# Weighted sum of eight index heads: fp32 matmuls against diagonal weights in place of scalar-tensor operations

## The chip, the cores and the metric

The kernel runs on one core of one Trainium2 chip. The metric is the device time of one execution in microseconds; the median of the runs is quoted. A core has a matrix engine (TensorE, PE in the profile), a vector engine (VectorE, DVE), a scalar engine (ScalarE, ACT), a general engine (GpSimd, POOL) and a queue that issues DMAs (SyncE, SP). Each works through its own list of instructions in order; semaphores make one wait for another. Matmuls write to PSUM, from which DVE and ACT read.

## The reference, cut to what matters

The program is a two-layer decoder trunk on 1024 tokens of 1024 features: an RWKV-7 time mixing and a gated convolution FFN, then sparse attention and a second such FFN. Only the attention is touched. For each of eight blocks of 128 queries it scores all keys with eight small index heads, keeps the 256 best keys of each query, and attends to those:

```python
s_idx = jnp.einsum('bthd,bsd->bths', qi_b, k_idx)
score = jnp.einsum('bths,bth->bts', jax.nn.relu(s_idx), wi_b).astype(jnp.float32)
causal = key_pos[None, :] <= t_pos[:, None]
score = jnp.where(causal[None], score, -jnp.inf)
_, sel = lax.top_k(score, topk)
...
logits = jnp.einsum('bthc,btkc->bhtk', q_abs, kv_sel).astype(jnp.float32) * qk_scale
```

`wi_b` holds one weight for each query and index head. The second line, the sum over the heads h of weight times relu, is what the change computes in another way. `topk` is 256, so the blocks 0 and 1 (tokens 0 to 255) keep every key and need no scores.

## The kernel before, in words

The attention (`dsa`) holds queries on the 128 partitions and keys along the free dimension. Block b sees W = 128 (b + 1) keys. `indexer(b)` scores blocks 2 to 7: for each slice of up to 512 keys and each head, PE makes two fp32r products into one PSUM bank (tile `si`, lines 1471 and 1472), ACT writes its Relu to SBUF (`relu`, line 1474), and DVE multiplies it with the head's weight column of `widx` and adds it to the scores `sc` (line 1476 for the first head, line 1478 for the seven others). POOL then masks future keys (`affine_select`, line 1482).

`topk` finds the 256th best score of each query by a binary search in two halves of 16 steps each, first on the upper 16 bits of the scores (tile `top`), then on the lower (tile `low`). It handles two blocks side by side: of one, DVE counts the keys above the limit (line 1515); of the other, ACT does (line 1513). After each count DVE moves the limit (lines 1517 and 1518). Between the two halves stand some twenty small operations (lines 1520 to 1544).

`logits` makes four heads' logits on PE (`lg`), and DVE adds the mask (`cm`, from POOL at line 1622) and takes the row minimum (`p`, `mn`, line 1638); ACT takes the exponential (line 1643). `values` transposes the probabilities on PE (`tp`, line 1669), ACT copies them out (`ph`, line 1677), PE multiplies by the values in plain fp32 (`ol`, line 1682) and by the output weights (`ops`, line 1687). `qabs` prepares the queries of 256 tokens (`qa`). Scores, logits and `qa` take turns in four PSUM banks of tag `l`.

The main line is attention in 32 units of four heads. Beside it a generator mixes in the rest: blocks 2, 3 and 4 are scored first, then units 0 to 6 run with the selection of blocks 2 and 3, block 5 is scored, units 7 to 14 run with the 32 head steps of blocks 6 and 7 and the selection of blocks 4 and 5, and units 15 to 22 run with the selection of blocks 6 and 7. The order in which instructions stand on each engine is made by a scheduler with a cost model of its own, from the order in which the program emits them and the buffers that are free.

The code below is that of the kernel before.

Of the kernel before, what the change touches and what calls it, by code (L numbers as in the profile page):

```python
# [30 lines left out]
class Ctx:  # L31
    """Handles shared by the phases."""


class Rows:
    """A [1024, 1024] DRAM array held as tiles of 128 rows."""

# [12 lines left out]
def split(k, raw, hi, lo, hi_eng="a", lo_eng="p"):  # L50
    """raw = hi + lo, each within float32r's digits."""
    nc = k.nc
    if hi_eng == "a":
        nc.scalar.copy(hi, raw)  # L54
    elif hi_eng == "v":
        nc.vector.tensor_copy(hi, raw)
    else:
        nc.gpsimd.tensor_scalar(hi, raw, 1.0, 0.0, ALU.mult, ALU.add)
    eng = nc.vector if lo_eng == "v" else nc.gpsimd
    eng.tensor_tensor(lo, raw, f32(hi), ALU.subtract)  # L60
# [9 lines left out]
def rstd_of(k, pool, var, n, eps, scale=1.0, tag="rs"):  # L70
    """(var * scale + eps) ** -0.5 on [128, n]"""
    nc = k.nc
    ve = pool.tile([128, n], F32, name="ve", tag=tag + "v", bufs=2)
    nc.vector.tensor_scalar(ve, var, scale, eps, ALU.mult, ALU.add)
    rs = pool.tile([128, n], F32, name="rs", tag=tag + "r", bufs=2)
    nc.gpsimd.tensor_tensor(rs, ve, k.mhalf[:, :n], ALU.pow)
    return rs


def layer_norm_rows(k, pool, res, g, b, out, eng="pp", sums=None, junk=None):  # L80
    """out[128, 1024] = LN(res) * g + b; res and out are lists of two [128, 512] tiles, sums [128, 2] the sums of res if
    they are known."""
    nc = k.nc
# [36 lines left out]
def wsplit(k, u, ap, n=512, lo_eng="v", raw=None):  # L120
    """DRAM block [128, n] -> hi, lo tiles"""
    raw = (raw or u)("wr")[:, :n]
    lo, hi = u("wl", F32R)[:, :n], u("wh", F32R)[:, :n]
    k.nc.sync.dma_start(raw, ap)
    split(k, raw, hi, lo, "a", lo_eng)
    return hi, lo


def out_z(k, acc, Z, z, g):
    """Feature-major hi, lo [128, 4, 512] of a 512-token half's g-th 512 features; z(tt, g) are token-major tiles."""  # L130
    zt = [z(tt, g) for tt in range(4)]
# [8 lines left out]
def residual(k, r, src, row, ch, ps):  # L140
    """r = ALPHA * src rows + ps"""
    k.nc.sync.dma_start(r, src[row : row + 128, ch * 512 : (ch + 1) * 512])
# [9 lines left out]
def out_proj(k, pool, u, raw, acc, res_tile, Z, w_ap, src, dst, hf, lnw):  # L152
    """dst rows of a 512-token half = LN(ALPHA * src + z @ w), Z = the two out_z of it; a generator of 16 products and
    4 normalisations."""
    res = {}
# [19 lines left out]
def out_proj_last(k, pool, u, raw, acc, acc1, wlate, nlate, res_tile, Z, w_ap, src, dst, hf, lnw):  # L175
    """out_proj whose rows are finished one tile of tokens after the other; Z[1] is only used after the third step.
    wlate has room for the split weights of the last nlate products."""
    a = {}
# [44 lines left out]
def interleave(main, n, *sides):  # L223
    """n steps of main with m steps of each (side, m) spread between them."""
    done = [0] * len(sides)
# [19 lines left out]
class Pools:  # L245
    """Pools that a phase opens and closes at its own points."""

# [23 lines left out]
def rwkv(k, src, dst):  # L271
# [74 lines left out]
    def mixed(hf, kt, n, xx=None, eng="p"):  # L346
        """hi, lo of x + (shift(x) - x) * mix[n] for one 128-feature tile."""
        xT = st[hf]["xT"]
# [56 lines left out]
    def prefetch(hf, n, g, m):  # L405
        """the first m operands of a projection to come"""
        for kt in range(m):
# [24 lines left out]
    def slot(ap, x):  # L432
        """first (k of BK, a of AR) or second (b of BK, r of AR) half of every 64-token chunk's 128 columns"""
        return ap.rearrange("p (c x i) -> p c x i", x=2, i=64)[:, :, x, :]
# [4 lines left out]
    def lora2(hf, g):  # L439
        """Decay and in-context rate gates; the rate waits in AR's a slots."""  # L440
        h_ = st[hf]
# [42 lines left out]
    def head_sums(ps, src_, i):  # L484
        """Token-major sums of src_ over the two heads of feature tile i."""
        for tt in range(4):
# [67 lines left out]
    def prep(hf, g, half):  # L554
        """Chunk matrices of 512 tokens x 8 heads, and the inverses (I - L)^-1 of their 64 x 64 triangles."""
        s = un[hf, g]
# [278 lines left out]
def ffn(k, layer, src, dst):  # L835
    """Both products go by Strassen-Winograd on 2 x 2 blocks: with
    S1 = A21 + A22, S2 = S1 - A11, S3 = A11 - A21, S4 = A12 - S2, T1 = B12 - B11, T2 = B22 - T1, T3 = B22 - B12,
    T4 = B21 - T2 and U = A11 B11 + S2 T2, V = U + S3 T3, the product's blocks are
    C11 = A11 B11 + A12 B21, C12 = U + S1 T1 + S4 B22, C21 = V + A22 T4, C22 = V + S1 T1."""
    nc, tc = k.nc, k.tc  # L840
# [19 lines left out]

    # x, feature-major: K halves by token halves
    X, raws = {}, {}
# [4 lines left out]
    def x_T(tt, ps):  # L867
        """ps() gives half a token tile's room"""
        pool = P_ if tt < 4 else L_
# [57 lines left out]
    def w_op(f, n, pool=None):  # L927
        """split operand n of the gate and value columns' tiles f"""
        w = W[f]
# [143 lines left out]

    # the second product: pairs of h's tiles, token halves by feature halves
    NPAIR = NF // 2
# [16 lines left out]
    def d_op(p, n, pool, lo_eng):  # L1092
        """operands of product n, both sides: hi and lo [128, 2, 512]"""
        r = R[p]
# [62 lines left out]
    def tail_op(f):  # L1157
        """a tile of h and its rows of the weights"""
        if layer == 1 and f == NF - 1:
# [61 lines left out]
def dsa(k, src, dst):  # L1221
# [41 lines left out]

    # absorbed query weights, scaled: w_uq[:, h] @ w_uk[h]
    wqk = k.dram.tile([8, 2, 128, 512], F32, name="wqk")
# [192 lines left out]
    def indexer(b):  # L1458
        """scores of block b's queries, future keys far below"""
        W = 128 * (b + 1)  # L1460
        s = M_.tile([128, W], F32, name=f"sc{b}")
        sc[b] = s
        lo = 256 if b < 4 else 512
        qs = slice(128 * b - lo, 128 * b - lo + 128)
        for n0 in range(0, W, 512):
            n1 = min(W, n0 + 512)
            n = n1 - n0
            for h in range(8):
                ps = acc("si")
                q_ = QS[lo][:, h, qs]  # L1470
                nc.tensor.matmul(ps[:, :n], q_, XTh[:, 3, n0:n1], start=True, stop=False)
                nc.tensor.matmul(ps[:, :n], q_, XTl[:, 3, n0:n1], start=False, stop=True)
                r = u("relu")
                nc.scalar.activation(r[:, :n], ps[:, :n], AF.Relu)
                if h == 0:
                    nc.vector.tensor_scalar(s[:, n0:n1], r[:, :n], widx[:, b, 0:1], 0.0, ALU.mult, ALU.add)
                else:
                    nc.vector.scalar_tensor_tensor(
                        s[:, n0:n1], r[:, :n], widx[:, b, h : h + 1], s[:, n0:n1], ALU.mult, ALU.add
                    )  # L1480
                yield
        nc.gpsimd.affine_select(
            s[:, W - 128 :], s[:, W - 128 :], pattern=[[-1, 128]], compare_op=ALU.is_ge, fill=-3e38, base=0,
# [5 lines left out]
    def topk(blocks):  # L1489
        """sc[b] <- 0 where the key is among the row's TOPK best, else NEG. The TOPK-th best is found bit by bit: first  # L1490
        the upper, then the lower half of the scores' bits, mapped to integers in the scores' order."""
        tag = f"_{blocks[0]}"
# [11 lines left out]
        def search(s, keys, first, lim):  # L1504
            """16 steps to c = the largest integer with no less than the limit's keys at or above it; the scalar
            engine sums the signs of keys - c + 1/2"""
            W, act, cnt, v = s["W"], s["act"], s["cnt"], s["v"]
# [65 lines left out]
    def qabs(pr, g):  # L1573
        """absorbed queries of 256 tokens, 8 heads: [128 c, hi/lo, head, token]"""
        Q = big("Q", (128, 2, 8, 256))
# [29 lines left out]
    def logits(b, g, g4):  # L1605
        """unnormalised softmax of four heads' logits"""
        W = 128 * (b + 1)
# [42 lines left out]
    def kv_split():  # L1650
        """kv's hi and lo, four key tiles each, in the room of the selection"""
        for i in range(2):
# [71 lines left out]
    def attention(u0, u1, n1):  # L1724
        """values of units u0 .. u1 - 1, logits up to unit n1 - 1"""
        for n in range(u0, u1):
# [48 lines left out]
    def wlate(name, dt=F32):  # L1775
        """a [128, 512] tile of the room that the queries and the probabilities leave"""
        if name == "wr":
# [118 lines left out]
def drive(phases):  # L1896
    """A phase starts (up to its first yield) before the one in front of it ends (from its last yield on)."""
    for i, ph in enumerate(phases):
# [28 lines left out]
```

## Time and profile before

| What | Value |
|---|---|
| device time, median of 3 runs | 3272.94 us (3261.83 to 3287.3) |
| span of the profiled execution, first to last instruction | 3266.9 us (its own total time is not given) |
| PE matmul busy | 2878.4 us, 88% |
| PE weight loads busy | 2257.1 us, 69% |
| DVE busy | 2620.8 us, 80% |
| ACT busy | 1492.1 us, 46% |
| POOL busy | 1718.2 us, 53% |
| first and last score product (line 1472) | 1893.4 and 2121.0 us |

Times within the execution count from its first instruction. Busy time is that of an engine's instructions, overlaps counted once. The table by stretch gives the busy time of PE, of its weight loads, of DVE, ACT and POOL in that order, each with the number of records in brackets, then the granted TensorE clock as a share of full speed. In a timeline a row has the start, the length, the engine, line, operation, tiles (out<-in), shape and the number of records that it merges. A plain fp32 matmul leaves two records.

### The profile page before, as it was taken

The page shows a single profiled execution, that of the slowest core. Times are in us where ns is not written, and L with a number is a line of the kernel's source. Part 1 is how long each engine was busy: PE and PEld are TensorE (multiplying, and loading weights), DVE is VectorE, ACT ScalarE, POOL GpSimd, SP SyncE. Part 2 cuts the span into 40 slices and gives each one's busy share as a digit, 9 for nine tenths or more (in the row PEclk, how much of TensorE's full clock was granted, in tenths as well). Part 3 has the DMA queues.
Part 4 walks back from the last instruction along what each step waited for, and adds up shares of the span by engine and source line. Part 5 has one row for each costly group of instructions (what it writes and reads, how often), then busy time and mean ns, then how long its engine had stood idle before and what let it go on. Part 6 is the DMA issues. An engine that isn't in the chain of part 4 may idle for free. (4 is left out here: it accounts for less than half of the span.)

```text
span 3266.9 us, 41699 instructions
## 1 busy us (share of the span) xinstructions
PE 2878.4 (88%) x15096; PEld 2257.1 (69%) x15096; DVE 2620.8 (80%) x4015; ACT 1492.1 (46%) x2571; POOL 1718.2 (53%) x1105
## 2 busy tenths in 40 slices
PE   6879869988898899999779888888999899999798
PEld 4667647766686677777667766656777677777577
DVE  7897897888847788888876779998475788888965
ACT  4545445454223444444222567876363444444222
POOL 5735445446124676666666622121313676766766
PEclk8889979989889899999889879999999899999889
DMA  2111111112216232236211611112214222235212
GB/s 79 61 40 43 58 36 38 57 33 62 94 56 206 78 84 77 78 83 210 101 65 35 217 40 65 62 33 86 81 51 155 71 78 78 78 91 206 77 52 91
DMA packets 187842, 268.36 MB, mean 82 GB/s; under 512 B 11914, under 2 KB 105482, under 8 KB 187250
## 3 DMA queue, kind: packets, MB, share of 16 engines
q1 hardware_dynamic: 187634, 265.69, 25.2%
q8 instruction: 119, 1.95, 0.2%
q14 instruction: 89, 0.73, 0.1%
HBM read 212.82 MB, written 52.82 MB: 81 GB/s over the span
## 5 line engine op out<-in xcount | busy, mean ns | idle before, releaser
L60 POOL TENSOR_TENSOR wo<-wr,wo 128x512 fp32r<-128x512 f32 x220 | 413.9, 1905 | 284.2 <-ACT wo L54 276.2
L990 DVE SCALAR_TENSOR_TENSOR cv<-u,vec,cv 128x1023 f32<-128x1023 f32 (+1 forms) x176 | 348.0, 1995 | 52.9 <-ACT cv L985 51.1
L60 POOL TENSOR_TENSOR xml<-xm,xmh 128x512 fp32r<-128x512 f32 x132 | 202.0, 1542 | 225.4 <-ACT xmh L54 215.7
L65 PE MATMUL dn<-dh 128*128 128x512 f32 x532 | 221.4, 416 | 66.3 <-DVE acc L1117 66.1
L60 POOL TENSOR_TENSOR dl<-raw,dh 128x1024 fp32r<-128x1024 f32 x82 | 219.2, 2696 | 104.7 <-ACT dh L54 104.4
L66 PE MATMUL dn<-dl,dh 128*128 128x512 f32 x532 | 218.8, 411 | 13.2 <-POOL dl L60 6.7
L65 PE MATMUL p<-xT,wo 128*128 128x512 f32 x528 | 215.1, 407 | 17.1 <-ACT u L974 11.3
L1622 POOL TENSOR_TENSOR cm<-sc,toep 128x256 f32<-128x256 f32 x96 | 75.8, 795 | 293.4 <-DVE mn L1638 225.1
L985 ACT ACTIVATE cv<-u,vec 128x1024 f32<-128x1024 f32 x88 | 109.5, 1244 | 252.7 <-DVE u L979 252.1
L67 PE MATMUL dn<-dh,dl 128*128 128x512 f32 x532 | 218.7, 411 | 0.0
L67 PE MATMUL p<-xT,wo 128*128 128x512 f32 x528 | 210.7, 399 | 4.6 <-POOL wo L60 4.6
L66 PE MATMUL p<-xT,wo 128*128 128x512 f32 x528 | 211.0, 400 | 3.0 <-DVE xT L60 3.0
L1117 DVE SCALAR_TENSOR_TENSOR acc<-acc,dn 128x512 f32<-128x512 f32 x196 | 131.0, 681 | 87.9 <-PE dn L67 87.9
L60 POOL TENSOR_TENSOR wo<-S,wo 128x512 fp32r<-128x512 f32 x88 | 175.4, 2013 | 30.7 <-ACT wo L54 30.7
L54 ACT CAST dh<-raw 128x1024 fp32r<-128x1024 f32 x95 | 94.7, 1046 | 201.7 <-PE dn L67 87.6
L60 POOL TENSOR_TENSOR wl<-wr,wh 128x512 fp32r<-128x512 f32 x84 | 121.6, 1448 | 119.8 <-ACT wh L54 84.8
L65 PEld LDWEIGHTS dn<-dh 128*128 128x128 f32 x532 | 106.0, 199 | 97.2 <-DVE acc L1117 41.5
L54 ACT CAST xmh<-xm 128x512 fp32r<-128x512 f32 x144 | 88.9, 617 | 114.4 <-DVE xm L353 35.5
L65 PE MATMUL p<-x,wo 128*128 128x512 f32 x352 | 139.2, 396 | 1.7 <-DVE x L60 1.3
L65 PEld LDWEIGHTS p<-xT,wo 128*128 128x128 f32 x528 | 100.3, 190 | 57.3 <-ACT u L974 27.2
L54 ACT CAST wo<-wr 128x512 fp32r<-128x512 f32 x220 | 127.2, 618 | 27.2 <-POOL wo L60 18.8
L66 PE MATMUL p<-x,wo 128*128 128x512 f32 x352 | 138.4, 393 | 0.0
(426 smaller groups left out, 9076.6 us busy)
## 6 DMA issues: line engine op xcount, KB each, us to landing
wr<-in_w_up_dram SPq DMA_DIRECT2D x88, 512.0 KB, 5.9
wr<-in_w_rkv_dram SPq DMA_DIRECT2D x96, 256.0 KB, 2.6
hd<-cv SPq DMA_DIRECT2D x44, 512.0 KB, 3.4
raw<-hd SPq DMA_DIRECT2D x19, 1024.0 KB, 4.9
raw<-in_w_down_dram SPq DMA_DIRECT2D x19, 1024.0 KB, 7.9
wr<-in_w_wo_dram SPq DMA_DIRECT2D x68, 256.0 KB, 2.8
acc<-x SPq DMA_DIRECT2D x16, 512.0 KB, 6.1
wh<-wqk SPq DMA_DIRECT2D x32, 256.0 KB, 3.0
```

Source lines behind the costliest of these rows:

```text
L54: nc.scalar.copy(hi, raw)
L60: eng.tensor_tensor(lo, raw, f32(hi), ALU.subtract)
L65: mm(ps, lhs[0], rhs[0], start=start, stop=False, **kw)
L66: mm(ps, lhs[0], rhs[1], start=False, stop=False, **kw)
L67: mm(ps, lhs[1], rhs[0], start=False, stop=stop, **kw)
L985: nc.scalar.activation(o, u, AF.Identity, bias=k.vec[:, cb : cb + 1], scale=k.vec[:, cw[2] : cw[2] + 1])
L990: nc.vector.scalar_tensor_tensor(o[:, d:], u[:, : 1024 - d], k.vec[:, cw[j] : cw[j] + 1], o[:, d:], ALU.mult, ALU.add)
L1117: nc.vector.scalar_tensor_tensor(o, o, ALPHA if first else 1.0, ps, ALU.mult, ALU.add)
L1622: (nc.vector if CFG["cm"][h4] == "v" else nc.gpsimd).tensor_tensor(cm[:, :near], mk, toep[g][:, h % 8, 256 - near :], ALU.add)
```

## The change

The weighted sum goes to PE. For each block POOL builds eight 128x128 diagonal matrices, the identity times one head's weight column, in two tiles `dg` of four (two POOL operations). After the Relu of head h, PE multiplies the diagonal of head h - 2 by that head's Relu, in plain fp32, and accumulates over the eight heads in one PSUM bank (`st`, from the same four banks of tag `l`). After the last head one DVE copy takes the sum to `sc`. The Relu stays on ACT, the mask on POOL. The diff also takes out comments and docstrings all over the file, which moves line numbers below the indexer by 10; it is cut here to the indexer.

```diff
     def indexer(b):
...
+        dg = [qr("dg").rearrange("p (a b) -> p a b", a=4) for _ in range(2)]
+        for i in range(2):
+            nc.gpsimd.tensor_tensor(
+                dg[i], k.ident[:, None, :].to_broadcast([128, 4, 128]),
+                widx[:, b, 4 * i : 4 * i + 4, None].to_broadcast([128, 4, 128]), ALU.mult,
+            )
         for n0 in range(0, W, 512):
             n1 = min(W, n0 + 512)
             n = n1 - n0
+            tot, rs = acc("st"), {}
+
+            def weigh(h):
+                nc.tensor.matmul(tot[:, :n], dg[h // 4][:, h % 4], rs.pop(h)[:, :n], start=h == 0, stop=h == 7)
+
             for h in range(8):
...
-                r = u("relu")
+                r = rs[h] = u("relu")
                 nc.scalar.activation(r[:, :n], ps[:, :n], AF.Relu)
-                if h == 0:
-                    nc.vector.tensor_scalar(s[:, n0:n1], r[:, :n], widx[:, b, 0:1], 0.0, ALU.mult, ALU.add)
-                else:
-                    nc.vector.scalar_tensor_tensor(
-                        s[:, n0:n1], r[:, :n], widx[:, b, h : h + 1], s[:, n0:n1], ALU.mult, ALU.add
-                    )
+                if h >= 2:
+                    weigh(h - 2)
                 yield
+            weigh(6)
+            weigh(7)
+            nc.vector.tensor_copy(s[:, n0:n1], tot[:, :n])
```

The scheduler sets the lists of the engines anew. On DVE, where the first softmax minimum of attention stands (unit 0, `p,mn<-lg,cm`), the list of the kernel before reads as follows; `sc_14783` is block 4's scores, and `cj,cnt` is a count of the search of block 3, on the upper halves (`top`).

```order
L1517 TENSOR_SCALAR v_2_14666<-cnt_2_14665 128x1
L1515 TENSOR_SCALAR cj,cnt_2_14684<-top,c_2_14683 128x512
L1478 SCALAR_TENSOR_TENSOR sc_14783<-relu,widx,sc_14783 128x128
L1518 TENSOR_SCALAR c_2_14664<-v_2_14666,c_2_14664 128x1
L1478 SCALAR_TENSOR_TENSOR sc_14783<-relu,widx,sc_14783 128x128
L1517 TENSOR_SCALAR v_2_14685<-cnt_2_14684 128x1
L1478 SCALAR_TENSOR_TENSOR sc_14783<-relu,widx,sc_14783 128x128
L1638 ISA p,mn<-lg,cm 128x128
```

In the changed list the same place reads as follows, with block 4's scores named `sc_14795` and their sum in PSUM `st`.

```order
L1525 TENSOR_SCALAR cj,cnt_2_14696<-low,c_2_14695 128x512
L1527 TENSOR_SCALAR v_2_14697<-cnt_2_14696,need_2_14702 128x1
L1491 COPY sc_14795<-st 128x128
L1527 TENSOR_SCALAR v_2_14678<-cnt_2_14677,need_2_14683 128x1
L1528 TENSOR_SCALAR c_2_14695<-v_2_14697,c_2_14695 128x1
L1528 TENSOR_SCALAR c_2_14676<-v_2_14678,c_2_14676 128x1
L1648 ISA p,mn<-lg,cm 128x128
```

The accumulation is gone from the list, and the search is further on: it counts on the lower halves (`low`). Before, 11 counts of block 3's search stand ahead of the first minimum; now 21 do.

On PE, at the end of block 7's scores and just ahead of the logits of unit 16, the list of before holds these rows.

```order
L1682 MATMUL ol<-ph,kv 128x512 x2
L1471 MATMUL si<-XTh,QS 128x512
L1472 MATMUL si<-XTl,QS 128x512
L1471 MATMUL si<-XTh,QS 128x512
L1472 MATMUL si<-XTl,QS 128x512
L1687 MATMUL ops<-wuv,ols 128x64 x4
L1471 MATMUL si<-XTh,QS 128x512
L1472 MATMUL si<-XTl,QS 128x512
```

The changed list holds these there.

```order
L1482 MATMUL si<-XTh,QS 128x512
L1483 MATMUL si<-XTl,QS 128x512
L1477 MATMUL st<-relu,dg 128x512
L1482 MATMUL si<-XTh,QS 128x512
L1483 MATMUL si<-XTl,QS 128x512
L1477 MATMUL st<-relu,dg 128x512 x3
L65 MATMUL lg<-XTh,Q 128x512
```

Each head's pair of products is now followed by one weighted product of an earlier head, and the last three stand together ahead of the logits.

## Rows read from the trace of the kernel before

**Rows 1.** busy time by stretch; from:to, length, busy us (records), PE clock, DMA
```profile
1893.00:1947.00 54.00, 40.95 (x188) 31.39 (x187) 45.24 (x136) 35.64 (x87) 6.31 (x8) 0.84 0.18 59
1947.00:1995.00 48.00, 43.88 (x280) 36.46 (x280) 45.50 (x219) 40.25 (x124) 16.82 (x29) 0.93 0.24 83
1995.00:2013.00 18.00, 15.35 (x87) 11.73 (x85) 17.96 (x52) 11.85 (x30) 3.65 (x5) 1.00 0.17 59
2013.00:2132.00 119.00, 98.37 (x480) 68.75 (x480) 116.73 (x424) 92.00 (x209) 27.25 (x35) 0.97 0.14 45
2132.00:2246.00 114.00, 98.16 (x508) 70.58 (x509) 108.19 (x395) 86.96 (x171) 23.18 (x30) 0.96 0.12 38
2380.00:2430.00 50.00, 49.99 (x278) 40.80 (x277) 39.52 (x122) 30.48 (x56) 10.37 (x15) 1.00 0.05 17
```

**Rows 2.** timeline of PE in D; start, length, engine, line, tiles, shape, records
```profile
2106.09 0.39 PE L1471 MATMUL si<-XTh,QS 128*128 128x512 f32 x1
2106.31 0.40 PE L1472 MATMUL si<-XTl,QS 128*128 128x512 f32 x1
...
2111.11 0.60 PE L1669 MATMUL tp<-ident,p 128*128 128x128 f32 x4
2111.54 1.02 PE L1682 MATMUL ol<-ph,kv 128*128 128x512 f32 x2
...
2113.30 1.02 PE L1682 MATMUL ol<-ph,kv 128*128 128x512 f32 x2
2114.16 0.60 PE L1669 MATMUL tp<-ident,p 128*128 128x128 f32 x4
```

**Rows 3.** groups by shape, PE, C and D; xcount, busy us, mean ns, idle
```profile
L1682 PE MATMUL ol<-ph,kv 128*128 128x512 f32 x62 | 33.3, 629 | 5.7 <-ACT ph L1677 5.6
L1669 PE MATMUL tp<-ident,p 128*128 128x128 f32 x120 | 20.1, 283 | 0.3 <-ACT p L1643 0.3
...
L66 PE MATMUL qa<-XTl,wh 128*128 128x256 f32 x34 | 10.0, 295 | 0.0
L1687 PE MATMUL ops<-wuv,ols 128*128 128x64 f32 x72 | 9.7, 278 | 1.8 <-ACT ols L1684 1.6
```

**Rows 4.** busy time by stretch of L1478 alone, then of L1476
```profile
1893.00:1947.00 54.00, 15.84 (x25) 0.84 0.18 59
1995.00:2013.00 18.00, 8.49 (x14) 1.00 0.17 59
2013.00:2132.00 119.00, 21.27 (x28) 0.97 0.14 45
...
1893.00:2246.00 353.00, 4.97 (x10) 0.94 0.15 51
```

**Rows 5.** a copy out of PSUM by shape; instructions of L1420 on POOL
```profile
L341 DVE COPY xT<-pt 128x512 f32<-128x512 f32 x8 | 5.5, 688 | 4.9 <-PE pt L335 4.9
...
L1420 POOL TENSOR_TENSOR toep<-toep,c x8: 1038/1039/1042, 1859.3 to 1935.4; 128x512 f32<-128x512 f32 x8
```

**Rows 6.** instructions of L1472; min/median/max ns, first and last start, shapes
```profile
L1472 PE MATMUL si<-XTl,QS x80: 272/393/628, 1893.4 to 2121.0; 128*128 128x512 f32 x48, 128*128 128x384 f32 x16, 128*128 128x128 f32 x8, 128*128 128x256 f32 x8
```

**Rows 7.** timeline of DVE in A and at the start of B
```profile
1920.02 0.74 DVE L1515 TENSOR_SCALAR_CACHE_REDUCE cj<-top,c 128x512 int16<-128x512 int16 x1
...
1935.37 0.75 DVE L1515 TENSOR_SCALAR_CACHE_REDUCE cj<-top,c 128x512 int16<-128x512 int16 x1
...
1936.59 0.69 DVE L1452 TENSOR_TENSOR QS<-qi,QS 64x512 fp32r<-64x512 f32 x1
...
1947.30 0.29 DVE L1638 CUSTOM_DVE_ANT_0 p<-lg,cm 128x128 f32<-128x128 f32 x1
...
1957.73 0.20 DVE L1518 TENSOR_SCALAR c<-v,c 128x1 f32<-128x1 f32 x1
...
1962.78 0.15 DVE L1544 TENSOR_SCALAR need<-need 128x1 f32<-128x1 f32 x1
```

**Rows 8.** what PE's idle time before L1471 waited for; us, times
```profile
  ACT relu L1474: 8.4, 18
```

More of the change, by code (lines that the diff above doesn't have):

```diff
@@ L31 @@
 class Ctx:
+    pass
 class Rows:
```

## The prediction

> **What bounds the kernel now.** I read the tables by stretch first, then the timelines of VectorE and TensorE, then the groups by shape. Only the attention layer's indexer is edited, and its eighty pairs of score products lie between 1893 and 2121 us [rows 6]. [rows 1] cuts 1893 to 2246 us into five stretches. A (1893 to 1947): query blocks 2, 3 and 4 are scored, and the selection (top-k) of blocks 2 and 3 begins. B (to 1995): attention on blocks 0 and 1. C (to 2013): block 5 is scored. D (to 2132): blocks 6 and 7 are scored head by head between the attention of blocks 2 and 3 and the selection of 4 and 5. E (to 2246): the selection of 6 and 7 beside the attention of 4 and 5. The reader is to see VectorE (DVE) busy 45.50 of 48 us in B, 17.96 of 18 in C, 116.73 of 119 in D and 108.19 of 114 in E: from the first search on it sets the pace. ScalarE (ACT) has 92.00 of 119 in D. PE's busy column reads 98.37 of 119 in D, and this is where the choice of measure matters.
>
> A matmul's row is longer than the place it takes. In [rows 2] two fp32r matmuls of 512 columns read 0.39 us each but start 0.22 apart (0.23 between most); four transposes take 0.43; one fp32 (not fp32r) product of 512 columns is two records and holds PE from 2113.30 to 2114.16, 0.86 us. Counting C and D that way from [rows 3]: 62 records of ol at 0.43 = 26.7; 120 transposes at 0.11 = 13.2; 102 qa (34 on each of three lines; 256 columns, half of 0.23) at 0.12 = 12.2; 72 ops, as short as a transpose, at 0.11 = 7.9; the logits of blocks 2 and 3, sixteen heads each with three products of 384 or 512 columns, 48 x 0.17 + 48 x 0.23 = 19.2, and block 4's first few 2; the score products of blocks 5, 6, 7, (32 x 0.23 + 8 x 0.17 + 8 x 0.12) x 2 = 19.4. Together 101 of 137 us, where the busy column sums to 113.7.
>
> **What it removes, adds and moves.** Removed from DVE: 70 scalar-tensor operations, 15.84 + 8.49 + 21.27 us in A, C and D plus a 1.3 us remainder at the start of B, and 10 tensor-scalar ones, 4.97 us [rows 4]; 51.9 in all. Added to DVE: ten copies of the sums out of PSUM, whose nearest row is a 128x512 copy out of PSUM at 0.69 us [rows 5]: six long ones 4.1, two of 384 columns about 1.1, the 256 and 128 about 0.7; 5.9. Net -46 us of DVE.
> Added to PE: eighty fp32 products with the shapes that [rows 6] lists (48 of 512 columns, 16 of 384, 8 of 256, 8 of 128). At 0.86 for 512 and in proportion: 48 x 0.86 + 16 x 0.65 + 8 x 0.43 + 8 x 0.22 = 41.3 + 10.4 + 3.4 + 1.8 = 57 us. By stretch: A 20.8 (blocks 2, 3, 4), C 10.3, D 25.8. So PE takes on more than DVE gives up.
> Added to POOL: twelve multiplications that build the diagonals; the nearest row, also 128x512 with one operand repeated, is 1.04 us [rows 5], 12.5 us in all. POOL is busy 27.25 of 119 us in D, so I cost them at nothing; if they were late, PE's first product of a block would wait. ACT keeps its eighty Relus.
> New waits: a weighted product waits for the Relu two heads back, and everything behind it on PE waits too; the copy on DVE waits for the block's last product, and the selection steps and softmax minima behind it wait with it. The sum also holds one of the four PSUM banks that scores, logits and qa share.
> Moved: in DVE's list the first softmax minimum (p) of attention now stands behind 21 steps of the search of block 3 where it stood behind 11, and so behind the work between that block's two searches (both lists are shown above). SP keeps its instructions, with a few stores of z a few places away.
>
> Now stretch by stretch.
> A. From the first search step (1920.02) to the first p (1947.30) DVE needed 27.3 us [rows 7]. Off it: block 4's accumulation before p, 11 of A's 25 operations, 15.84 x 11/25 = 7, and its two first heads, 0.5 each [rows 4]. On it: ten more steps at 1.22 (1935.37 to 1936.59), the work between the searches at 4 (1957.73 to 1962.78 less 1 us that belongs to others), two qa splits that used to come earlier 1.4, copies 0.9. 27.3 - 8 + 12.2 + 4 + 1.4 + 0.9 = 37.8: +10.5. The 12.1 us of products for blocks 2 and 3 lie ahead of the search; PE is idle 13 of 54 us in A by its busy column, so I let 2.5 of them through (bounds 0 and 9). A: +13, between +8 and +20.
> B. The ten steps and the work between, 16 us, and the 1.3 are gone from DVE, which leaves 28 of 45.5. PE does what it did: 43.88 by the busy column, about 39 if that shrinks as in C and D (101/113.7). With 40 for the stretch: -7 to -8, I take -7; bounds -9 and -3.
> C and D. DVE: 134.7 - 8.49 - 21.27 - 3 (its share of the 4.97) + 3.6 = 105. PE: 101 + 36 = 137, the whole of the 137 us that the stretches last now. PE becomes the bound. In 2380 to 2430, where nothing else binds, it reads 49.99 of 50 [rows 1]; among the waits for ACT here I expect 95%: 137 / 0.95 = 144, +7. Bounds 0 (no gap at all) and +15 (90%).
> E. No indexer work lies here; a few us of small DVE operations stand earlier in the list now. -3, bounds -6 and 0.
> Sum: 13 - 7 + 7 - 3 = **+10 us**, bounds -7 and +32. After 2246 us PE's order is the one of before. The profiled span is 3266.9, so the sum gives a span of 3277; the shown runs' median, 3272.94, is 6.0 above that span (the profiled execution's own total is not given), so I predict 3283 us.
>
> A rule speaks against counting PE like this. The Trainium skill (Perfetto Trace Analysis, section Identifying the Most-Contended Engine) calls matmul busy share a bad measure of PE's headroom, which the 0.39 against 0.23 bears out, and puts the busy share of weight loads in its place. By the busy column C and D would need 113.7 + 36 = 150 us, +13 instead of +7. By the weight loads, 11.73 + 68.75 of 137 or 59%, PE would have room for all of it and the stretch would follow DVE down to 107 us, -30. I take neither: an fp32 product holds PE 0.86 us for two loads, so loads undercount it.
>
> **Rivals.** (1) *PE packs without gaps.* DVE's relief then shows: A +8, B -9, C and D 0, E -6, so -7: 3266 us. For it: DVE is what PE waited for in the front part, and its load falls by a seventh. Against it: ACT at 92 of 119 stays, and PE waits for ACT more than for DVE there. In the extreme of PE never binding, as weight loads would have it, the sum is 13 - 7 - 30 - 3 = -27: 3246 us.
> (2) *The weighted products stand waiting for ACT* (slower). In D PE's queue is one file of logits, transposes, values and weighted products; a Relu that comes late holds all of it, where before only DVE waited. For it: PE already lost 8.4 us in 18 waits for Relu, 0.47 each [rows 8], and ACT's own queue holds the searches' sign passes. At 0.47 for D's 32 products 15 us are added, 3298; at 1 us each 32, 3315. From about 0.7 us each on it decides the sign beyond what can be told. Against it: between a Relu and its product stand two heads' scores, 0.92 us of PE work, and in A and C a head of 512 columns costs PE 2 x 0.23 + 0.86 = 1.3 us with nothing of attention between, which leaves ACT time for one Relu.
> (3) *Half clock.* A's granted clock is 0.84 [rows 1]; if PE's longer work in A falls in a half-clock span, 14 us of block 4 become up to 28, and A is +20 or more: 3290 us. It is inside the range.
>
> **How the numbers follow.** My forecast, PE bound in C and D and the front part longer, with (3) in it: 0.53, 3276 to 3293. Rival 1: 0.22, of which the extreme has 0.05. Rival 2: 0.22. 0.03 for what I don't see. The range runs from 3255 to 3316: below it lies the extreme of rival 1 and a little more, above it the worst of rival 2. One per cent, 33 us (about what runs of this kernel can tell from no change), puts the borders at 3240 and 3306. Faster by that: 0.04, half of rival 1's extreme and of what I don't see. Slower: 0.16, rival 2 from 0.7 us on and the worst of A. Within: 0.80.
>
> **What would show it.** In the profile after: DVE's operations on the scores gone and ten copies of 0.3 to 0.7 us there; 160 more PE records, 0.43 us apart at 512 columns; first p at about 1960; DVE near 105 of C and D's 144 and PE without idle time; E still DVE's. If D is shorter than 119 us, PE was not the bound and rival 1 holds; if PE shows idle time in front of the weighted products with Relu as the releaser, rival 2. If the first p comes at 1947 or earlier, my reading of DVE's list is wrong.

## The result, and the profile after

The changed kernel took 3318.26 us, median of four runs (3299.45 to 3331.82), against 3267.39 us for the kernel before: a ratio of 1.0127 (the two medians alone give 1.0156), 95% interval 1.0081 to 1.0173, or 26 to 57 us slower. The forecast was 3283 us and 10 us slower: the direction was right, the size a fifth to a quarter of what came; the median lies 2 us above the range's upper end, while the median of the kernel before is here 6 us below the one that the forecast started from.

All of it lies between two points that any profile shows: the start of the second product of the indexer's first pair of score products on TensorE (PE, line 1472 before, 1483 after) and the last softmax minimum on VectorE (DVE, line 1638, then 1648). Call this the stage. The tables below cut it at the first minimum, at block 5's first score product and at the last score product; the four stretches answer to A, B, C with D, and E of the prediction, only that E runs on to the last minimum. Of the profiles below, that of the kernel with blocks 2 to 4 alone is of a slow execution (3315.06 us; its fastest took 3264.9). The columns are those of [rows 1]. First the kernel before, at these cuts:

```profile
1893.40:1947.30 53.90, 40.85 (x188) 31.31 (x186) 45.52 (x136) 35.92 (x89) 6.31 (x8) 0.84 0.18 59
1947.30:1997.60 50.30, 46.14 (x291) 37.87 (x291) 47.83 (x231) 41.88 (x127) 17.55 (x30) 0.93 0.26 87
1997.60:2121.00 123.40, 103.02 (x516) 73.89 (x515) 121.13 (x445) 97.16 (x228) 26.95 (x34) 0.97 0.15 49
2121.00:2445.00 324.00, 292.13 (x1482) 220.37 (x1480) 241.76 (x737) 185.30 (x345) 76.61 (x87) 0.97 0.18 61
```

The changed kernel:

```profile
1891.70:1964.10 72.40, 60.79 (x245) 41.84 (x245) 50.19 (x193) 42.89 (x108) 13.05 (x15) 0.89 0.13 44
1964.10:2016.80 52.70, 48.51 (x307) 40.36 (x307) 35.22 (x167) 37.90 (x114) 17.88 (x31) 0.92 0.24 78
2016.80:2158.70 141.90, 131.55 (x598) 87.65 (x597) 110.73 (x405) 98.08 (x223) 31.98 (x41) 1.00 0.13 44
2158.70:2490.20 331.50, 299.13 (x1488) 225.71 (x1486) 231.11 (x716) 183.74 (x341) 74.33 (x84) 0.95 0.18 59
```

The stage grew from 551.7 to 598.5 us: A +18.5, B +2.4, C and D +18.5, E +7.5. PE's busy column rose by 20 in A and 28.5 in C and D; DVE fell to 110.73 of 141.90 us and no longer fills any stretch.

What one weighted product costs is as forecast. In block 5's scoring, where nothing else is on PE (timeline of PE, columns as [rows 2]):

```profile
2019.92 0.79 PE L1482 MATMUL si<-XTh,QS 128*128 128x512 f32 x1
2020.56 0.39 PE L1483 MATMUL si<-XTl,QS 128*128 128x512 f32 x1
2020.79 1.02 PE L1477 MATMUL st<-relu,dg 128*128 128x512 f32 x2
2021.24 0.80 PE L1482 MATMUL si<-XTh,QS 128*128 128x512 f32 x1
```

A head takes 1.32 us from XTh to XTh; two score products apart by 0.23 leave 0.86 for the weighted one. The 0.64 between XTh and XTl is then part of it: XTl starts late behind it, where two score products follow each other in 0.23 us. The other new operations cost what [rows 5] had, by line (min/median/max ns, first and last start, shapes):

```profile
L1467 POOL TENSOR_TENSOR dg<-ident,widx x12: 1038/1040/1041, 1882.1 to 2113.4; 128x512 f32<-128x512 f32 x12
...
L1491 DVE COPY sc<-st x10: 280/689/692, 1900.7 to 2161.7; 128x512 f32<-128x512 f32 x6, 128x384 f32<-128x384 f32 x2, 128x128 f32<-128x128 f32 x1, 128x256 f32<-128x256 f32 x1
```

The waits in A (waiting line, what it waited for: us, times, longest) show DVE behind PE. On DVE:

```profile
DVE sc L1491 <- PE st L1477: 10.8, 2, 6.8
```

On PE:

```profile
PE si L1482 <- DVE QS L1452: 4.0, 2, 2.5
...
PE st L1477 <- DVE QS L1452: 2.4, 1, 2.4
...
PE st L1477 <- ACT relu L1485: 0.7, 2, 0.4
```

In C and D PE waited for Relus at the weighted products as follows:

```profile
PE st L1477 <- ACT relu L1485: 1.6, 2, 1.3
```

That is 2.3 us in all, not the 15 to 32 of rival 2 (and less than the 8.4 ahead of the score products before [rows 8]).

The selection, which was most of DVE's work in B, is earlier, yet nothing comes of it. In the kernel before the last count of block 3's search and the first minimum that needs block 2's selection are these (timeline of DVE):

```profile
2008.82 0.36 DVE L1560 TENSOR_SCALAR sc<-sc 128x384 f32<-128x384 f32 x1
...
2013.44 0.26 DVE L1638 CUSTOM_DVE_ANT_0 p<-lg,sc 128x128 f32<-128x128 f32 x1
```

The first row finishes block 2's mask, 4.6 us ahead of its use. In the changed kernel:

```profile
2021.63 0.35 DVE L1570 TENSOR_SCALAR sc<-sc 128x384 f32<-128x384 f32 x1
...
2033.73 0.29 DVE L1648 CUSTOM_DVE_ANT_0 p<-lg,sc 128x128 f32<-128x128 f32 x1
```

Now it is 12.1 us early: DVE's selection is not what this minimum waits for, before or after.

### The profile page after: what moved, and what is told of

Read it like the earlier page. It is cut to its first block, busy times and chain, and to the rows that moved or that the text cites. A ratio compares the mean times of both kernels' runs of the same rounds, so it can differ in the third digit from the quotient of the medians.

```text
span 3312.8 us, 41940 instructions
## 1 busy us (share of the span) xinstructions
PE 2930.9 (88%) x15256; PEld 2283.7 (69%) x15256; DVE 2593.1 (78%) x3945; ACT 1494.4 (45%) x2571; POOL 1728.8 (52%) x1117
## 5 line engine op out<-in xcount | busy, mean ns | idle before, releaser
L65 PEld LDWEIGHTS dn<-dh 128*128 128x128 f32 x532 | 106.0, 199 | 97.8 <-DVE acc L1117 42.1
```

The costliest lines, as they stand in the source:

```text
L65: mm(ps, lhs[0], rhs[0], start=start, stop=False, **kw)
```

## The experiments

The theories. **1**: PE's list of instructions was already about as long as the time, so products added to it come through and DVE's relief is worth little. **2**: the sums in PSUM make DVE wait, and what stands behind the waiting copies is late. **3**: the new order on DVE costs the time. **4**: the sum takes away one of four PSUM banks. **5**: PE stands still for the Relu at each tail (the last two products of a slice follow their Relus at once).

**How far a difference can be trusted.** The kernel before, profiled again:

> The kernel before once more, for a second profile. All theories: the stage from the first score product to the last softmax minimum within 4 us of the 551.7 of the first profile, while the time ahead of it moves by up to 20 us.

```profile
1914.50:1968.40 53.90, 41.06 (x187) 31.36 (x186) 45.47 (x136) 35.89 (x89) 6.32 (x8) 0.87 0.18 59
1968.40:2018.90 50.50, 46.41 (x293) 37.90 (x292) 47.95 (x231) 42.07 (x127) 17.56 (x30) 0.94 0.26 88
2018.90:2142.20 123.30, 104.19 (x516) 75.07 (x515) 121.06 (x445) 97.17 (x228) 26.94 (x34) 0.96 0.15 49
2142.20:2465.80 323.60, 291.86 (x1482) 220.37 (x1480) 241.71 (x737) 185.38 (x345) 76.71 (x87) 0.97 0.18 61
```

The stage repeats to 0.4 us, 551.3 against 551.7, while it starts 21 us later. So the stage is the fine measure, and the totals, with intervals of 11 to 27 us to either side, the coarse one. That is one pair of profiles, though, and both have 51.2 us at PE's lower clock level (1.2 of 2.4 GHz) within the stage; the other kernels have 41.0 to 78.5. What moves the start is PE's clock. Ahead of the stage all kernels hold the same work; the quickest and the slowest of the profiles are these (from the program's start, columns as above), first the kernel with carried tails at three heads (below):

```profile
0.00:1871.80 1871.80, 1616.16 (x9426) 1272.67 (x9427) 1519.27 (x1843) 807.90 (x1322) 1069.82 (x681) 0.92 0.25 83
```

then the one with blocks 2 to 4 alone:

```profile
0.00:1919.10 1919.10, 1665.31 (x9426) 1311.04 (x9427) 1515.12 (x1843) 807.92 (x1322) 1066.72 (x681) 0.89 0.25 81
```

DVE, ACT and POOL do nearly the same busy time, PE does not. Over 14 profiles the time at 1.2 GHz ahead of the stage runs from 287 to 410 us, and the stage starts 0.39 us later for each microsecond of it (correlation 0.98; without the second of these two 0.41 and again 0.98). I use 0.39 as an estimate of the price of a microsecond at the lower level within the stage too, where the work is another.

**VectorE relieved, nothing added to PE.** The kernel before with:

```diff
-                else:
+                elif h == 7:
                     nc.vector.scalar_tensor_tensor(
```

> The kernel before with only heads 0 and 7 weighted and summed on VectorE; the other sixty scalar-tensor operations are left out (so the scores hold two heads of eight), nothing is added to TensorE. It takes about 40 us off VectorE in the scoring stretches, nearly what the change takes off it. Theory 1 (TensorE's list was already about as long as VectorE's, so VectorE's relief is worth little): 0 to -15 us against the kernel before. Theory 2 (VectorE set the pace, and what the change lost comes from new waits for the sums in PSUM): -25 to -40 us. Theory 3 (the new order on VectorE, more search counts ahead of the first softmax minimum, costs the time by itself): slower than before by 10 us or more if the relief moves the order the same way.

Ratio 0.9937 (0.9902 to 0.9972): 20 us faster, between theories 1 and 2. The stage says 10.0 us:

```profile
1910.70:1962.80 52.10, 38.35 (x185) 29.78 (x184) 40.96 (x153) 38.09 (x97) 6.42 (x9) 0.88 0.19 61
1962.80:2012.30 49.50, 46.13 (x293) 38.74 (x294) 41.80 (x195) 40.06 (x124) 17.61 (x30) 0.92 0.28 90
2012.30:2127.50 115.20, 101.64 (x515) 75.08 (x514) 107.51 (x415) 94.66 (x221) 25.85 (x34) 0.97 0.15 52
2127.50:2452.30 324.80, 289.82 (x1482) 220.17 (x1480) 237.86 (x728) 184.89 (x345) 78.79 (x87) 0.97 0.18 61
```

In B DVE lost 6 of its 47.83 us and the stretch 0.8. DVE was full there, but with counts that were not yet needed. C and D gave back 8.2 us, A 1.8. And the order: here 16 counts of block 3's search stand ahead of the first minimum (11 before, 21 in the change), with no loss. That speaks against theory 3, with half of the shift.

**The products cheaper.** The changed kernel with:

```diff
-        dg = [qr("dg").rearrange("p (a b) -> p a b", a=4) for _ in range(2)]
+        dg = [qr("dg", F32R).rearrange("p (a b) -> p a b", a=4) for _ in range(2)]
...
-                r = rs[h] = u("relu")
+                r = rs[h] = u("relu", F32R)
```

> The changed kernel with the Relus and the diagonals written as fp32r, so that a weighted product is one pass (0.23 us at 512 columns by the pairs of score products) in place of 0.86; the sums are less exact, everything else stays, the copies out of PSUM too. TensorE's added work falls from 57 to about 16 us. Theory 1: 35 to 45 us below the changed kernel, within 10 us of the kernel before. Theory 2: the waits of the copies stay, 5 to 20 us below the changed kernel. Theory 3: the order stays, so within 10 us of the changed kernel.

Ratio 1.0064 (1.0030 to 1.0097); the stage 568.3 us, 30.2 below the changed kernel for 41 us of PE work less. That speaks for theory 1, though 16.6 us above the kernel before is more than it allows for. It speaks against theory 3, which expected no gain: 19 counts stand ahead of the first minimum here, nearly as many as in the change. A, then C and D:

```profile
1909.70:1972.90 63.20, 47.49 (x216) 37.27 (x215) 46.44 (x175) 41.46 (x104) 13.53 (x15) 0.84 0.15 51
...
2027.40:2155.00 127.60, 112.34 (x552) 83.17 (x551) 107.17 (x401) 97.55 (x223) 28.98 (x38) 0.95 0.14 49
```

**The products doubled.** Each weighted product is issued twice into the same sum:

```diff
+                r_ = rs.pop(h)[:, :n]
+                for i_ in range(2):
+                    nc.tensor.matmul(tot[:, :n], dg[h // 4][:, h % 4], r_, start=h + i_ == 0, stop=h + i_ == 8)
```

> The changed kernel with every weighted product issued twice into the same sum, which doubles all scores and leaves the selection as it is. TensorE gets another 57 us, and nothing else changes. Theory 1: the added time comes through nearly whole, 45 to 57 us above the changed kernel, some 90 to 105 above the kernel before. Theory 2: only the two products at each sum's end lie in a wait, 10 sums x 2 x up to 0.86 = 17 us above the changed kernel at most. Theory 3: under 10 us above the changed kernel as long as the order does not move.

Ratio 1.0281 (1.0241 to 1.0322); the stage 649.5 us, 51.0 above the changed kernel, as theory 1 had it, and three times what theory 2 allowed:

```profile
1887.40:1982.20 94.80, 82.10 (x317) 55.41 (x315) 60.95 (x238) 48.86 (x125) 13.78 (x16) 0.89 0.10 34
...
2033.40:2205.10 171.70, 163.17 (x688) 104.96 (x687) 111.55 (x405) 98.97 (x223) 31.67 (x41) 1.00 0.11 37
```

A took 22.4 us more for 20.8 of products, C and D 29.8 for 36. DVE's waits for the sums over the whole stage, in the change and then here, grew by 28.2 us, so they alone don't make the 51.0:

```profile
DVE sc L1491 <- PE st L1477: 25.3, 6, 6.8
...
DVE sc L1493 <- PE st L1479: 53.5, 5, 12.8
```

**The front alone.** Blocks 2 to 4 summed on PE, 5 to 7 on DVE:

```diff
+        pe = b < 5
...
-                if h >= 2:
+                if pe and h >= 2:
                     weigh(h - 2)
```

> The change for blocks 2, 3 and 4 alone (32 of the 80 weighted products, 20.8 us of TensorE); blocks 5, 6 and 7 are summed on VectorE as before. Theory 1: the first softmax minimum 15 to 18 us later, as in the changed kernel, and nothing lost after it: 10 to 20 us above the kernel before. Theory 2: the waits of the four copies of these blocks, 10.8 us, so about as much, with the rest (14.5 us of waits) gone. Theory 3: most of the loss, 30 us or more, since the order around the first minimum is that of the change.

Ratio 1.0017 (0.9979 to 1.0054); the stage 571.8 us, 20.1 above before, of which 18.4 in A and none from block 5's scores on. So the loss adds up by blocks, and theory 3 falls, since the order around the first minimum is that of the change. The totals are 7 us lower to 18 higher than before, a little less than the 20.1 of this one profile.

**A bank held, without the sum.** Two heads on VectorE as above, and:

```diff
+            hold = acc("st")
...
+                if h in (0, 7):
+                    nc.tensor.matmul(hold[:, :64], k.ident, r[:, :64], start=h == 0, stop=h == 7)
+                if h == 7:
+                    nc.vector.tensor_copy(u("held")[:, :64], hold[:, :64])
```

> The kernel with two heads summed on VectorE (the other six left out), in which each slice also holds a bank of PSUM from head 0 to head 7, as the changed kernel's sum does: two plain fp32 products of 64 columns, one at head 0 and one at head 7, and a copy of 64 columns. TensorE gets about 4 us, VectorE about 2. With one pass of fp32r per weighted product the stage from the first score product to the last softmax minimum was 26.6 us longer than with two heads on VectorE, for 15.7 us of products. Theory 4 (one of four banks taken away, and the copy's wait, cost the rest): 10 to 15 us above the kernel with two heads, in the stage and in the total. Theory 1 (TensorE's time alone): 0 to 6 us above it.

Ratio 1.0093 (1.0053 to 1.0133); the stage 565.0 us, 23.4 above two heads on VectorE. It does not settle theory 4, for it brought in another wait: its products follow their Relus with no head in between. PE's waits in A:

```profile
PE st L1483 <- ACT relu L1475: 11.3, 6, 7.7
```

**The last head's product alone**, in fp32r (it starts and ends its sum, as `start` and `stop` are both set):

```diff
-                if h >= 2:
-                    weigh(h - 2)
...
-            weigh(6)
             weigh(7)
```

> The changed kernel with one weighted product for each slice, that of head 7, in fp32r; heads 0 to 6 are left out of the sum. Ten products, 2 us of TensorE; the ten copies stay whole and each waits for the last head's Relu and product; the bank is held only from that product to the copy. Theory 1: as the kernel with two heads on VectorE, within 6 us, so 10 to 25 us below the kernel before. Theory 2 (the copies' waits and what stands behind them on VectorE cost the rest): 10 to 20 us above the kernel with two heads.

Ratio 1.0056 (1.0019 to 1.0093); the stage 561.1 us, 19.5 above two heads on VectorE for 2 us of products and ten copies. It fits neither 1 nor quite 2: half of it, 10.1 us, is in A, where DVE waited 5.6 us for sums and PE

```profile
PE st L1477 <- ACT relu L1485: 6.3, 4, 2.6
```

and A's granted clock was 0.77 against 0.88, 17 us more at the lower level. That led to theory 5.

**The copies on ScalarE.**

```diff
-            nc.vector.tensor_copy(s[:, n0:n1], tot[:, :n])
+            nc.scalar.copy(s[:, n0:n1], tot[:, :n])
```

> The changed kernel with the ten copies out of PSUM on ScalarE in place of VectorE, so that VectorE's list no longer stops for a sum. Theory 2: VectorE waited 25 us for the sums there, and 8 us of TensorE's waits for QS came behind them; with the waits gone 10 to 25 us below the changed kernel. Theory 1: TensorE's list is as long as before, so within 6 us of the changed kernel, and ScalarE's exponentials may stand behind the copies: up to 5 us slower.

The stage is 589.1 us, 9.4 shorter, but A, where VectorE's wait was longest, went from 72.4 to 72.8, and half of the 9.4 lies in E, where the clock was 0.96 against 0.95. In A the wait moved and did not go. A search can't begin before its scores, and DVE now waited for `top`, which ACT makes of block 3's scores behind the copy and the mask:

```profile
1909.80:1982.60 72.80, 60.42 (x247) 42.00 (x247) 49.66 (x195) 45.02 (x114) 13.22 (x15) 0.89 0.13 44
...
DVE cj L1538 <- ACT top L1537: 9.1, 1, 9.1
```

So this run does not decide theory 2. The total, 1.0184 (1.0143 to 1.0226), is not lower: it stands 10 us or more above what the stage says. In the profiled execution that lies ahead of the stage, which starts at 1909.8 us against 1891.7 in the change, with the same work and 372 us at 1.2 GHz against 335; of the other three there is no profile.

**The tails carried** into the next slice, in plain fp32 and in fp32r with two and with three heads between Relu and product (the last run changes the 2 to 3):

```diff
+                late.append(partial(weigh, h, r))
+                if len(late) > 2:
+                    late.pop(0)()
...
+        while b not in (2, 6) and late:
+            late.pop(0)()
```

> The changed kernel, plain fp32, with the tails carried into the next slice in the same way. TensorE waited only 2.3 us for Relus in the changed kernel, since a plain fp32 product leaves ScalarE 0.86 us, but VectorE waited 25 us for the sums. Theory 1: the stage within 5 us of the changed kernel's. Theory 5: 0 to 3 us shorter. Theory 2 (VectorE's waits for the sums): 10 us or more shorter.

> One pass of fp32r per weighted product, as before, but the last two products of a slice and its copy are issued behind the first two heads of the next slice (or block) wherever one follows at once: six of the ten tails no longer stand right behind their Relu; blocks 3, 4, 5 and 7 keep theirs. With the tails in place TensorE waited 8.6 us for Relus and VectorE as much for the sums, and the stage from the first score product to the last softmax minimum was 16.6 us longer than before. Theory 5 (TensorE's list stands still for the Relu at each tail, and that is what the sum in PSUM costs beyond its products): the stage 6 to 12 us shorter than with the tails in place. Theory 1 (TensorE's time): the same products, within 4 us.

> As the fp32r kernel with carried tails, the products three heads behind the Relu in place of two. Theory 5: another 0 to 4 us off the stage, and the nearest of these to the kernel before; if the 10 us that VectorE's relief gave by itself come through, at or under its time. Theory 1: no change.

Plain fp32: ratio 1.0144 (1.0061 to 1.0227), the stage 589.3 us, 9.2 below the changed kernel; 2.7 of it in C and D, and 6.6 in E, where no product was changed:

```profile
2173.70:2498.60 324.90, 293.35 (x1488) 222.03 (x1486) 230.91 (x715) 183.41 (x341) 74.36 (x84) 0.97 0.18 61
```

The clock is 0.97 here and 0.95 in the changed kernel, 20.5 and 34.1 us at the lower level: 13.6 x 0.39 = 5.3 of the 6.6. The minima of E bear it out: counted from the last score product, the changed kernel falls behind this one by 2.5 us up to the 25th microsecond, 1.2 more up to the 90th and 2.7 more between the 155th and the 219th, and in these places it has 6.8, 3.4 and 3.4 us more at the lower level. So E's +7.5 was mostly clock (not all such differences are: the doubled kernel's E is 331.8 us with 27.3 at the lower level). In fp32r: ratios 1.0083 (1.0042 to 1.0125) and 1.0038 (0.9994 to 1.0082), the stage 566.4 and 561.8 us, that is 1.9 and 6.5 below the tails in place. PE's waits for Relus at the products, over the stage, with the tails in place, carried, and carried at three heads:

```profile
PE st L1477 <- ACT relu L1485: 8.7, 8, 3.0
...
PE st L1484 <- ACT relu L1496: 7.9, 6, 3.0
...
PE st L1484 <- ACT relu L1496: 2.6, 3, 1.0
```

DVE's waits for the sums, with the tails in place and carried:

```profile
DVE sc L1491 <- PE st L1477: 8.6, 3, 3.6
...
DVE sc L1486 <- PE st L1484: 3.6, 2, 2.3
```

The first step hardly touched the wait that theory 5 means, so its 6 to 12 us could not come; the second took 5.3 us of it away and 4.6 off the stage. Theory 5 is right about the wait, and it is a small part. The first step also took 5.0 us off DVE's waits, and the stage gave 1.9, less than the clock alone (71.7 and 58.0 us at the lower level) would make of it. That speaks against theory 2, with the doubled kernel.

**A way around PE.** The kernel before, with GpSimd taking the first two heads (three in blocks 6 and 7):

```diff
+                if h < (3 if b > 5 else 2):
+                    wb = widx[:, b, h : h + 1].to_broadcast([128, n])
+                    nc.gpsimd.tensor_tensor(r[:, :n] if h else s[:, n0:n1], r[:, :n], wb, ALU.mult)
+                    if h:
+                        nc.gpsimd.tensor_tensor(s[:, n0:n1], r[:, :n], s[:, n0:n1], ALU.add)
```

> The kernel before with the first two heads of each slice (three in blocks 6 and 7) weighted and summed on GpSimd, by a multiplication and an addition, and the rest on VectorE; nothing on TensorE. It takes 24 of 80 operations, about 15 us, off VectorE, and gives GpSimd 38 operations of about 1 us. Theory 1, with the relief of VectorE at the measured 20 us for sixty operations: 24/60 of it, 8 us below the kernel before, less what GpSimd's slower chain holds up in blocks 2 to 5, where the heads come 0.5 to 1.3 us apart: 0 to -8 us. The rival: VectorE waits for GpSimd's part at each slice, 10 slices x 2 to 3 us, and it is slower by 5 to 15 us.

Ratio 1.0010 (0.9972 to 1.0048), the stage 564.6 us, 12.9 longer: in the stage the rival was right in size. An addition of 512 columns took 1.37 us in C and D, but DVE waited only 5.3 us for GpSimd's part, not the rival's 20 to 30; another 6.8 us at the lower level make 2.7 by the estimate above, and the rest is open. No version here that sums all eight heads is faster than the kernel before.

**The sum over the runs.** Relief of DVE: -10.0 with 47.8 us at the lower level in the stage, against 51.2 before, so -8.7 at equal clock. To this I add the products (forecast rates) and 0.39 us for each microsecond at the lower level beyond 51.2.

| Kernel | products | at 1.2 GHz | sum | measured |
|---|---|---|---|---|
| last head alone, fp32r | 2.0 | 78.5 | +3.9 | +9.5 |
| fp32r | 15.8 | 71.7 | +15.1 | +16.6 |
| fp32r, carried | 15.8 | 58.0 | +9.8 | +14.7 |
| fp32r, carried, three heads | 15.8 | 54.6 | +8.4 | +10.1 |
| the change | 57 | 58.0 | +51.0 | +46.8 |
| copies on ScalarE | 57 | 47.8 | +47.0 | +37.4 |
| fp32, carried | 57 | 41.0 | +44.3 | +37.6 |
| doubled | 114 | 54.6 | +106.6 | +97.8 |

Cheap products come out 2 to 6 us above the sum (Relus, sums), long ones 4 to 10 below (a sixth at most of the products finds room). Theory 1 holds within that: it is the products, nearly whole. The held bank is not in the table; with 4 us of products and 75.1 at the lower level the sum gives +4.6 for it, and +13.3 was measured, with 13.2 us of waits for Relus. Theory 4 was not tested by itself. In the kernel carried at three heads a sum holds its bank at least as long as in the change, and only 1.7 us are left above the sum, so there the bank can't cost much.

## Why the prediction was right in direction and wrong in size

The direction came for a reason that was given (PE becomes the bound of C and D); that A landed inside its bounds is luck, since it was summed on the wrong list. Two steps failed: DVE was taken for the pace of A and B, and PE's gaps in C and D were taken for room.

- **The price of a product, 57 us in all**: right (0.86 us; 20.8 more in A gave 22.4).
- **"From the first search on it sets the pace" (DVE)**: this failed. DVE was 95 to 98% busy, but much of it was search, which could wait. The Trainium skill (Perfetto Trace Analysis, section Identifying the Most-Contended Engine) takes VectorE's busy share as a fair measure of how close it is to its roofline (the most that it could do). Here the share did not tell what relief is worth: in B, 95% busy, 6 us less work brought 0.8.
- **A, +13 (8 to 20)**: +18.5, inside. It was summed on DVE's list, where PE's, with its waits, was the path (doubling the products lengthened A by 22.4 us): I let 2.5 us of the 12.1 for blocks 2 and 3 through, and 9.3 came: block 4's first score product starts 45.4 us into the stage, 36.1 before.
- **B, -7 (-9 to -3)**: +2.4, wrong sign. DVE's busy time there fell by 12.6 us and none of it came through. PE counted by the same rates has 40 of 50.3 us before, and lies partly at the lower level (0.93). That its list, with its waits, was the path already is argued from this; shown is that DVE's was not.
- **C and D, +7 (0 to +15)**: +18.5. This is the largest mis-sized term. I let the 36 us fill PE's gaps up to 95%. Counted as in the prediction, from block 5's first score product to the last, PE holds 92.4 of 123.4 us before (75%), 92.2 of 115.2 with VectorE relieved (80%), 124.6 of 141.9 in the change (88%) and 157.9 of 171.7 doubled (92%). The gaps, in the main waits of PE's own list for ACT and DVE, shrink but do not close when work is added: 23.0 us with VectorE relieved, 17.3 in the change, 13.8 doubled. Against the relieved kernel 26.7 of the 36 us came through.
- **E, -3 (-6 to 0)**: +7.5, mostly the clock; at the clock of before +0.9 (carried fp32).
- **Rival 1 and the weight-load measure**: out. The doubled kernel has PE's weight loads at 104.96 of 171.70 us, 61%, as the changed one has 62%, while the time followed PE's work.
- **Rival 2**: the wait exists and is small, 2.3 us: a plain fp32 product of 0.86 us leaves ACT time for a Relu (median 0.58 us). Where the product is cheap or follows its Relu at once it is larger: 3.0 to 11.3 us in A.
- **Rival 3**: A's clock was 0.89, higher than before; it had no part in A. The order (21 counts ahead of the first minimum) was read rightly; no run shows a cost of it.

## What to carry to other kernels

Ask of a full engine whether its work is due: take the work off, in an experiment that leaves it out, before you pay for it elsewhere. Gaps in an in-order engine's list that are waits of its own chain are little room for new work: here three quarters (C and D) to all (A) of the added products came through, so count them nearly whole unless the trace shows an idle stretch that ends for another reason. Measure a local change between two instructions that stand at its ends: the clock ahead of the stage moved its start by 47 us over these profiles, while the stage of the kernel before repeated to 0.4. Then look at the clock within it as well. And when a run is to remove a wait, read in its trace that the wait is gone: the copies on ScalarE only moved it.

## What the runs showed of the hardware

The same work ahead of the stage took from 1871.80 us at a mean granted clock of 0.92 to 1919.10 us at 0.89, and the time followed the microseconds at 1.2 GHz (correlation 0.98). In C and D the clock rose from 0.97 to 1.00 with the products added, and PE idled less by its busy column (20.4 us, then 10.3). A cheaper product can bring a wait back: in A PE waited 3.0 us for Relus with fp32r and 0.7 with plain fp32, with 19.9 us at 1.2 GHz against 15.3.
